# First FFN product of two half layers by quarters, with seven products for eight

## The chip, the cores and the metric

The kernel runs on one core of a Trainium2 chip. Its time is the device time of one execution in microseconds (us); lower is better. TensorE (PE) multiplies, VectorE (DVE) and ScalarE (ACT) work elementwise, GpSimd (POOL) and SyncE (SP) issue DMAs here.

## The reference, cut to what matters

A decoder of two layers, one with retention and one with sliding-window attention, runs one step for a prompt of 1024 tokens and a sample of 8 × 4 tokens. Each layer ends with a feed-forward part (FFN); the model's width is 1024, the FFN's 4096, all in float32.

```python
def rms_norm(x, g):
    xf = x.astype(jnp.float32)
    y = xf * lax.rsqrt(jnp.mean(xf * xf, axis=-1, keepdims=True) + EPS)
    return y.astype(x.dtype) * g.astype(x.dtype)

def ffn(h, g_pre, w1, w2, g_post):
    u = jax.nn.relu(rms_norm(h, g_pre) @ w1)
    return h + rms_norm((u * u) @ w2, g_post)
```

## The kernel before, in words

Activations lie feature by feature: 128 features on the partitions, tokens along the columns. Tokens go in two halves: half 0 has 512 (one piece), half 1 has 544 (two pieces of 272, the sample's 32 among them). A float32 product is made of three passes of a rounded format: each operand is split into a high part (a cast) and a low part (the rest), and `passes` (L343) gives high·high, high·low and low·high. Every accumulation over 1024 inputs is thus 8 × 3 matmuls.

`load_w` (L309) brings weights: for each block two DMAs of 128 x 1024 on SP's queue (L318), a cast on ScalarE for `whi` (L328), a subtraction on VectorE for `wlo` (L329). `proj_fm` (L346) multiplies: the matmul is L356, and after each pair of inputs it calls `tick` (L359).

`Ffn.up(i)` (L740) makes 256 of the 4096 features: two columns of 128, in half 0 as 2 × 24 = 48 matmuls of 512 columns, in half 1 as 96 of 272; ScalarE takes Relu out of PSUM (L748) and squares (L749), POOL stores the block to DRAM (`uD`, L751). `ups(a, b)` runs blocks a to b-1 of 16. `Ffn.downs` is the second product: it fetches `uD` by POOL (L756), cuts it into high and low parts (L763, L764), multiplies through `proj_fm`, and sums chunks on VectorE (`acc_out`, L362 to L367). PSUM has one pool: four banks tagged mm, four tagged aux.

The order of the work is the program's, with side work woven in. A side is a generator, such as `norms` (L280: it fetches `h` by POOL, takes `norm_r` with two matmuls by ones at L265 and L266, VectorE and ScalarE passes, and makes the next input's high part at L305 and its low part at L306). `tick` adds the work's size times a rate from the table `RATES` (L156) and runs a step of the first side for each whole unit; `drain` runs what is left. A scheduler may still shift instructions when the program is built. Around the change the main order is: the retention layer, in whose last part blocks 0 to 2 of `f0` run; then `f0` (half 0, layer 0), `f1` (half 1, layer 0), `fa` (half 0, layer 1) and `f2` (half 1, layer 1), each ups and then downs. Beside `f1.downs` and `fa.downs` run the sides of the attention of half 0 and half 1 (`at`, `smp`, `wo`, `lt`), whose last one makes the input of the next FFN. Beside `f0.ups` runs `norms` of half 1 (side f0), and beside `f2.ups` the norm and the output of half 0 (sides fo).

Of the kernel before, what the change touches and what calls it, by code (L numbers as in the profile page):

```python
# [116 lines left out]
def body(ctx, tc,  # L117
# [31 lines left out]
    def yt(w=TM, dt=F32):
        return yp.tile([P, w], dt, tag="y", bufs=16, name="y")  # L150
# [10 lines left out]
    def side(gen, rate=None):  # L161
        sides.append((gen, rate))
# [88 lines left out]
    def norm_r(get, w):  # L251
# [95 lines left out]
    def passes(a, b):  # L347
        return [(a[0], b[0]), (a[0], b[1]), (a[1], b[0])]
# [383 lines left out]
    class Ffn:  # L732
# [6 lines left out]
        def up(self, i):  # L739
# [10 lines left out]
            s_ = 2 * (i % 2)  # L750
            G.dma_start(out=uD[self.half][:, 2 * i:2 * i + 2], in_=self.st[:, s_:s_ + 2, :t_])  # L751

        def fetch(self, j):
            hi, lo = x4(), x4()
            t_ = TT[self.half]
            G.dma_start(out=f32(lo)[:, :, :t_], in_=uD[self.half][:, 4 * j:4 * j + 4])  # L756
            self.parts[j] = (hi, lo)

        def cut(self, j):
            t_ = TT[self.half]  # L760
            hi, lo = (t[:, :, :t_] for t in self.parts[j])
# [450 lines left out]
            S.activation(out=sel[:, i], in_=sel[:, i], func=AF.Copy, scale=den[:, i:i + 1])  # L1212

    def swa_sides(sw, half, am=None, skr=None):
        xs = []

        def late():
            xs.extend(xs_alloc())
            yield from norms(half, sw.y, g_spost, xs=xs, pre=g_f1)

        side(sw.attend(), f"at{half}")
        if half:
            side(sw.attend_sample(am, skr), "smp")
        side(sw.wo(), f"wo{half}")
        side(late(), f"lt{half}")
        return xs

    CHUNKS = [1, 2, 2, 2, 1]
    with tc.tile_pool(name="rp", bufs=1) as rp:
        G.dma_start(out=g_first, in_=gsrcs[0].rearrange("(k p) -> p k", p=P))  # L1230
# [4 lines left out]
        rets = [Ret(0, [(hi[k // 4][:, k % 4], lo[k // 4][:, k % 4]) for k in range(KT)], rp), None]  # L1235
        for _ in range(RATES["w0"]):
            next(ini)
        first = rets[0].qk_w(0, 0)
        run(ini)
        for g in (gen, x_store(0, loads), x_store(1)):  # L1240
            side(g, "x")
        qk = rets[0].qk(0, [[(0, 256)], [(256, 256)]], first)
        drain()
        prev = None
        for half in range(2):
            r = rets[half]
            for h in range(RH):
                pace[0] = RATES["vg"][half]
                last = h == RH - 1
                vs = r.v(h)  # L1250
                if last:
                    drain()
                    prev[0].wout(*prev[1:])
                    prev = None
                    xs = xs_alloc()
                    norm = norms(1 - half, xs=xs, pre=g_f0 if half else g_rpre)
                    side(norm, "n1")
                sg = r.g(h)
# [111 lines left out]
```

## Time and profile before

| | us |
|---|---|
| three runs | 2905.68, 2906.42, 2906.97 (median 2906.42) |
| profiled execution, its own time | 2905.74 |
| its span, first to last instruction | 2903.9 |
| TensorE busy in the span | 2849.2 |
| VectorE busy | 1526.7 |
| ScalarE busy | 1264.1 |

The profile lists for each group of instructions its line, engine, operation and tile, output <- input, with the partitions and columns. A busy time is the union of the instructions' own times; matmuls overlap one another, so the distance from start to start is shorter than the duration of one. A granted clock of 1.00 is 2.4 GHz, of 0.50 is 1.2 GHz. In a timeline, square brackets give the idle time of the engine before the row and what ended it.

### The profile page before, as it was taken

What the parts mean: (1) busy time and instruction counts of PE and PEld (TensorE: products, weight loads), DVE (VectorE), ACT (ScalarE), POOL (GpSimd) and SP (SyncE); (2) the same over time, 40 slices, a digit from 0 to 9 for tenths busy, and PEclk for the clock granted to TensorE, in tenths of its full rate; (3) what the DMA queues carried; (4) which work ended last, traced back from release to release, by engine and by line L of the source; (5) the groups of instructions that cost most, each with busy time, mean ns of one, the idle gap of its engine ahead of it and who ended that gap; (6) DMA issues with size and microseconds to landing.
All of it is one profiled execution on the core that took longest, in us unless ns stands there. A gap on an engine that the chain in (4) does not pass through costs nothing.

```text
span 2903.9 us, 42531 instructions
## 1 busy us (share of the span) xinstructions
PE 2849.2 (98%) x16989; PEld 2487.6 (86%) x16989; DVE 1526.7 (53%) x3045; ACT 1264.1 (44%) x2554; POOL 177.3 (6%) x262
## 2 busy tenths in 40 slices
PE   8999999999999999999999999999999999899998
PEld 7888888888989788888998898978877788899998
DVE  5444565576566644553444664654357535542345
ACT  3343353343325444432545764445458533444322
POOL 2000000011010100000000000000010100000000
PEclk9999999999999999999999999999999999899999
DMA  6322332455263645553554333355432434346432
GB/s 206 93 83 89 95 113 87 157 169 176 91 209 97 219 144 173 179 152 98 163 165 131 126 96 95 109 164 163 156 128 87 131 94 150 105 148 217 157 103 68
DMA packets 418420, 391.08 MB, mean 135 GB/s; under 512 B 13878, under 2 KB 360286, under 8 KB 416174
## 3 DMA queue, kind: packets, MB, share of 16 engines
q1 hardware_dynamic: 380191, 248.97, 29.0%
q0 software_dynamic: 36848, 137.36, 13.3%
q8 instruction: 133, 2.18, 0.3%
q10 hardware_dynamic: 1183, 2.04, 0.2%
q14 instruction: 65, 0.53, 0.1%
HBM read 308.73 MB, written 79.56 MB: 134 GB/s over the span
## 4 chain that ended last, share of the span: by engine, by line
PE 88%; issue 4%; DVE 3%; DMA 2%; ACT 2%; POOL 0%; SPq 0%; DVEq 0%; ACTq 0%; POOLq 0%
PE mm L356 66%; PE mm L496 6%; PE mm L940 5%; PE aux L629 2%; PE aux L638 2%; DMA wraw<-in_ffn_w_dram 1%; PE aux L705 1%; PE aux L1098 1%; PE aux L714 1%; PE aux L547 1%; PE aux L573 1%; PE aux L1065 1%; PE aux L496 1%; DVE wlo L329 0%; ACT whi L328 0%
## 5 line engine op out<-in xcount | busy, mean ns | idle before, releaser
L356 PE MATMUL mm<-x,whi 128*128 128x272 f32 (+2 forms) x8768 | 1912.6, 325 | 11.9 <-DVE y L367 6.0
L356 PEld LDWEIGHTS mm<-x,whi 128*128 128x128 f32 x8768 | 1381.7, 189 | 153.3 <-issue 9.8
L356 PE MATMUL mm<-x,wlo 128*128 128x272 f32 (+2 forms) x4384 | 1192.5, 324 | 0.0
L329 DVE TENSOR_TENSOR wlo<-wraw,whi 128x1024 fp32r<-128x1024 f32 x396 | 483.7, 1222 | 713.4 <-ACT whi L328 712.8
L328 ACT CAST whi<-wraw 128x1024 fp32r<-128x1024 f32 x396 | 415.4, 1049 | 938.2 <-PE mm L356 798.1
L356 PEld LDWEIGHTS mm<-x,wlo 128*128 128x128 f32 x4384 | 738.4, 189 | 62.1 <-DVE wlo L329 0.6
L367 DVE TENSOR_TENSOR y<-y,mm 128x272 f32<-128x272 f32 (+1 forms) x264 | 130.9, 516 | 182.5 <-PE mm L356 182.0
L496 PE MATMUL mm<-whi,x 128*128 128x512 f32 x512 | 166.9, 397 | 0.0
L940 PE MATMUL mm<-whi,x 128*128 128x512 f32 x384 | 124.2, 394 | 0.0
L496 PEld LDWEIGHTS mm<-whi,x 128*128 128x128 f32 x512 | 96.1, 189 | 22.8 <-DVE n L476 0.8
L496 PE MATMUL mm<-wlo,x 128*128 128x512 f32 x256 | 101.2, 395 | 0.0
L764 DVE TENSOR_TENSOR x<-x,x 128x1024 fp32r<-128x1024 f32 (+1 forms) x64 | 78.7, 1254 | 32.3 <-ACT x L763 32.1
L257 DVE TENSOR_TENSOR n<-n 128x272 f32<-128x272 f32 (+1 forms) x196 | 84.2, 430 | 10.7 <-ACT n L256 2.4
L749 ACT ACTIVATE x<-x 128x272 f32<-128x272 f32 (+1 forms) x192 | 88.5, 497 | 1.5
L940 PEld LDWEIGHTS mm<-whi,x 128*128 128x128 f32 x384 | 72.1, 188 | 17.6
L751 POOL DMA_DIRECT2D uD<-x x64 | 40.2, 628 | 746.4 <-ACT x L749 655.6
L748 ACT ACTIVATE x<-mm 128x272 f32<-128x272 f32 (+1 forms) x192 | 81.3, 457 | 3.6 <-PE mm L356 3.5
L763 ACT CAST x<-x 128x1024 fp32r<-128x1024 f32 (+1 forms) x64 | 66.8, 1076 | 22.1 <-DMA x<-uD 15.2
L940 PE MATMUL mm<-wlo,x 128*128 128x512 f32 x192 | 75.7, 394 | 0.0
L334 DVE SCALAR_TENSOR_TENSOR wlo<-wraw,gall,whi 128x512 fp32r<-128x512 f32 x48 | 34.6, 747 | 59.8 <-ACT whi L333 59.6
L496 PEld LDWEIGHTS mm<-wlo,x 128*128 128x128 f32 x256 | 48.4, 189 | 10.5
L333 ACT ACTIVATE whi<-wraw,gall 128x512 fp32r<-128x512 f32 x48 | 32.7, 717 | 54.5 <-PE aux L940 19.8
(310 smaller groups left out, 2531.8 us busy)
## 6 DMA issues: line engine op xcount, KB each, us to landing
wraw<-in_ffn_w_dram SPq DMA_DIRECT2D x256, 512.0 KB, 4.1
wraw<-in_ret_w_in_dram SPq DMA_DIRECT2D x96, 512.0 KB, 3.8
uD<-x POOLq DMA_DIRECT2D x32, 544.0 KB, 5.7
x<-uD POOLq DMA_DIRECT2D x16, 1088.0 KB, 7.4
wraw<-in_ret_w_out_dram SPq DMA_DIRECT2D x32, 512.0 KB, 3.5
x<-in_state_ret_dram SPq DMA_DIRECT2D x32, 512.0 KB, 5.3
out_dram<-x POOLq DMA_DIRECT2D x32, 512.0 KB, 3.4
uD<-x POOLq DMA_DIRECT2D x32, 512.0 KB, 5.7
```

The costliest lines, as they stand in the source:

```text
L257: V.tensor_tensor(out=acc, in0=acc, in1=sq, op=ALU.add)
L328: S.copy(out=hi, in_=raw)
L329: V.tensor_tensor(out=lo, in0=raw, in1=f32(hi), op=ALU.subtract)
L356: T.matmul(p_[:, :w], lhsT=a, rhs=b[:, o:o + w], start=(k == 0 and i == 0), stop=(k == n - 1 and i == 2))
L367: V.tensor_tensor(out=y[m][:, o:o + w], in0=y[m][:, o:o + w], in1=ps, op=ALU.add)
L496: T.matmul(ps[c][:a.shape[1]], lhsT=a, rhs=b, start=(k == 0 and i == 0), stop=(k == KT - 1 and i == len(prods) - 1))
L629: T.matmul(ps, lhsT=a, rhs=b, start=(n == 0), stop=(n == len(prods) - 1))
L748: S.activation(out=d, in_=ps, func=AF.Relu)
L749: S.activation(out=d, in_=d, func=AF.Square)
L763: S.copy(out=hi[:, a:a + 2], in_=f32(lo)[:, a:a + 2])
L764: V.tensor_tensor(out=lo[:, a:a + 2], in0=f32(lo)[:, a:a + 2], in1=f32(hi)[:, a:a + 2], op=ALU.subtract)
L940: T.matmul(ps[c][:a.shape[1]], lhsT=a, rhs=b, start=(k == 0 and i == 0), stop=(k == KT - 1 and i == len(prods) - 1))
```

## The change

The first FFN product of `f0` for blocks 5 to 15, and of `f2` for blocks 2 to 15, is made by another scheme (Winograd's form of Strassen's). A block's weights (1024 inputs, 256 features) and its input (1024 inputs, one half's tokens) are cut in quarters, A11 to A22 of the input by tokens (256 or 272 columns) and by inputs (512), and B11 to B22 of the weights. Seven products of 512 inputs, 128 features and 256 or 272 tokens replace eight. Each takes 4 × 3 = 12 matmuls, so a block takes 84. `Quarters.build` makes the sums S1 to S4 of the input once per half (14 VectorE operations and 4 casts, each of 1024 or 1088 columns) as a side `s7` during the two plain blocks ahead. `Seven` loads raw weights into a rotating tile (L354) and makes the sums T1, T3, T2 and T4 for each block: low parts at L370, sums at L373 (VectorE), casts on ScalarE at L377 (ha), L380 (h2), L387 (h1), L393 (hb) and L398 (h4). `seven` (L413) runs the products (matmul L429) and combines them: a copy u1 of the first product on ScalarE (L434), then on VectorE slot 0 (L437), slot 1 (L441), slot 2 (L444) and u2 (L446). `up7` takes Relu (L935) and Square (L936) of the whole block and stores it (L937). The blocks have a PSUM pool of their own, in which each product's tile has a single buffer: p1, px (two products), py (three) and p4.

The side f0 moves from `f0.ups` to `f0.downs`, the sides fo from `f2.ups` to `f2.downs`, and some rates change. In the new kernel `norm_r`'s matmuls are L272 and L273, `load_w`'s subtraction is L500 and `proj_fm`'s matmul L527.

```diff
-    RATES = {..., 'f0': 0.43, ..., 'at0': 2.4, 'wo0': 2.4, 'lt0': 2.4, 'at1': 3.25, 'smp': 3.25, 'wo1': 3.25, 'lt1': 3.25, 'fo': 0.43, ...}
+    RATES = {..., 'f0': 0.9, 's7': 1.25, ..., 'at0': 2.6, 'wo0': 2.6, 'lt0': 2.6, 'at1': 3.8, 'smp': 3.8, 'wo1': 3.8, 'lt1': 3.8, 'fo': 0.9, ...}
+    class Quarters:
...
+            def diff(r, a, b):
+                (ah, al), (bh, bl) = f[a], f[b]
+                V.tensor_tensor(out=r, in0=f32(ah), in1=f32(bh), op=ALU.subtract)
+                V.tensor_tensor(out=r, in0=r, in1=f32(al), op=ALU.add)
+                V.tensor_tensor(out=r, in0=r, in1=f32(bl), op=ALU.subtract)
...
+            diff(r0, "A22", "A21")
+            yield
+            minus(r1, r0, "A11")
+            yield
+            cut("S1", r0)
+            yield
+            minus(r0, r1, "A12")
+            cut("S2", r1)
+            yield
+            diff(r1, "A11", "A21")
+            yield
+            cut("S4", r0)
+            cut("S3", r1)
+            yield
...
+        def prep(self):
...
+            ha, la = pair()
+            f["B11"], f["B21"] = (ha[:, 0:4], la[:, 0:4]), (ha[:, 4:8], la[:, 4:8])
+            S.copy(out=ha, in_=raw[:, 0])
+            yield
+            h2, l2 = quarter("B22")
+            S.copy(out=h2, in_=b22)
+            low(ha, la, raw[:, 0])
+            yield
+            low(h2, l2, b22)
+            add(b11, b11, b12)
+            yield
+            h1, l1 = quarter("T1")
+            S.copy(out=h1, in_=b11)
+            add(b12, b12, b22)
+            add(b22, b11, b22)
+            yield
+            hb, lb = pair()
+            f["T3"], f["T2"] = (hb[:, 0:4], lb[:, 0:4]), (hb[:, 4:8], lb[:, 4:8])
+            S.copy(out=hb, in_=raw[:, 1])
+            add(b21, b22, b21)
+            low(h1, l1, b11)
+            yield
+            h4, l4 = quarter("T4")
+            S.copy(out=h4, in_=b21)
+            low(hb, lb, raw[:, 1])
+            yield
+            low(h4, l4, b21)
+            yield
...
+        p1 = pool.tile([P, 512], F32, tag="p1", name="p1")[:, :s]
+        px = pool.tile([P, 2, 512], F32, tag="px", name="px")[:, :, :s]
+        py = pool.tile([P, 3, 512], F32, tag="py", name="py")[:, :, :s]
+        p4 = pool.tile([P, 512], F32, tag="p4", name="p4")[:, :s]
...
+        prod(p1, "A11", "B11")
+        u1 = c[:, 3, :s]
+        S.copy(out=u1, in_=p1)
+        prod(px[:, 1], "S2", "T2")
+        prod(px[:, 0], "A12", "B21")
+        V.tensor_tensor(out=slot(0), in0=twice(u1), in1=px, op=ALU.add)
+        u2 = c[:, 0, s:2 * s]
+        prod(py[:, 1], "S3", "T3")
+        prod(py[:, 2], "S1", "T1")
+        V.tensor_tensor(out=slot(1), in0=twice(u2), in1=py[:, 1:3], op=ALU.add)
+        u3, v = c[:, 1, :s], c[:, 1, s:2 * s]
+        prod(py[:, 0], "S4", "B22")
+        V.scalar_tensor_tensor(out=slot(2), in0=twice(v), scalar=-1.0, in1=py[:, 0:2], op0=ALU.mult, op1=ALU.subtract)
+        prod(p4, "A22", "T4")
+        V.tensor_tensor(out=u2, in0=u3, in1=p4, op=ALU.add)
...
+        def ups7(self, a, b):
+
+            self.xq = Quarters(self.half, self.xs)
+            side(self.xq.build(), "s7")
...
+            self.up(a - 2)
+            w = [load(a)]
+            self.up(a - 1)
+            drain()
+            run(w[0].prep())
+            w.append(load(a + 1))
+            bank_pool("p7")
+            for i in range(a, b):
+                if i + 2 < b:
+                    w.append(load(i + 2))
+                if i == b - 2:
+                    self.fetch(0)
+                self.up7(i, w[i - a], w[i + 1 - a] if i + 1 < b else None)
+            bank_pool("pp")
+            self.cut(0)
...
+        f0.ups7(5, 2 * NFB)
         xs = xs_alloc()
         side(norms(1, rets[1].y, g_rpost, xs=xs, pre=g_f0), "f0")
-        f0.ups(3, 2 * NFB)
         f0.downs(CHUNKS)
...
-        f2.ups(0, 1)
+        f2.ups7(2, 2 * NFB)
...
-        f2.ups(1, 2 * NFB)
         f2.downs([2, 2, 2, 1])
```

First place: VectorE in the up blocks of `f0`. Before, it stands between norm steps (L257, L262, L303, L306) and the low parts of weights (L329):

```order
L329 TENSOR_TENSOR wlo<-wraw,whi 128x1024
L262 TENSOR_TENSOR n<-n 128x272
L329 TENSOR_TENSOR wlo<-wraw,whi 128x1024 x9
L269 TENSOR_TENSOR n<-n 128x272
L270 SCALAR_TENSOR_TENSOR n<-aux,n 128x272
L271 SCALAR_TENSOR_TENSOR n<-n 128x272
L303 SCALAR_TENSOR_TENSOR n<-x_9579,gall,n 128x272 x8
```

Now one block's rows, from its slot 0 on (x_9867 is the result, x_9736 the next block's raw weights, x_9860 those of the one after it):

```order
L437 TENSOR_TENSOR x_9867<-x_9867,px 128x512
L370 TENSOR_TENSOR wlo<-x_9736,whi 128x1024
L370 TENSOR_TENSOR wlo<-x_9860,whi 128x1024
L370 TENSOR_TENSOR y<-x_9736,y 128x512
L441 TENSOR_TENSOR x_9867<-x_9867,py 128x512
L373 TENSOR_TENSOR x_9860<-x_9860 128x512
L370 TENSOR_TENSOR y<-x_9736,y 128x512
L446 TENSOR_TENSOR x_9867<-x_9867,p_9866 128x256
L373 TENSOR_TENSOR x_9860<-x_9860 128x512
L444 SCALAR_TENSOR_TENSOR x_9867<-x_9867,py 128x512
L370 TENSOR_TENSOR y<-x_9860,y 128x512
L373 TENSOR_TENSOR x_9860<-x_9860 128x512 x2
```

Thirteen operations stand in one queue for each block; slot 1 (L441) has three low parts ahead of it: lb and l1 of the next block and la of the one after.

Second place: TensorE from one seven-product block to the next, in `f0` (p_10235 is the next block's p1, x_9566 is S4, x_9564 is S2):

```order
L429 MATMUL p_10235<-x_8290,whi 128x256
L429 MATMUL p_10235<-x_8292,whi 128x256
L429 MATMUL p_10235<-x_8290,wlo 128x256
L429 MATMUL py<-x_9566,y 128x256 x12
L429 MATMUL p_10235<-x_8290,whi 128x256
L429 MATMUL p_10235<-x_8292,whi 128x256
L429 MATMUL p_10235<-x_8290,wlo 128x256
L429 MATMUL p_10235<-x_8290,whi 128x256
L429 MATMUL p_10235<-x_8292,whi 128x256
L429 MATMUL p_10235<-x_8290,wlo 128x256
L429 MATMUL px<-x_9564,whi 128x256 x2
```

The product S4 of a block stands in the middle of P1 of the next one; before, a block was 48 matmuls of 512 columns at L356 with no other between.

Third place: TensorE where `fa.downs` (512 columns) meets `f2` (272 columns). Before, the two matmuls of the last norm stand inside `f2.up(0)`:

```order
L356 MATMUL mm<-x_22306,whi 128x272
L356 MATMUL mm<-x_22308,whi 128x272
L356 MATMUL mm<-x_22306,wlo 128x272
L265 MATMUL aux<-n,onesd 128x272
L266 MATMUL aux<-n,onesd 128x272
L356 MATMUL mm<-x_22305,whi 128x272 x3
```

Now they stand inside the last down product:

```order
L272 MATMUL aux<-n,onesd 128x272
L527 MATMUL mm<-x_22788,whi 128x512
L527 MATMUL mm<-x_22789,whi 128x512
L273 MATMUL aux<-n,onesd 128x272
L527 MATMUL mm<-x_22788,wlo 128x512
```

Behind L273 come 13 matmuls of 512 columns and then the first of 272. After that norm's first pair of matmuls came 174 matmuls of `fa.downs` before and 258 now; where `f1.downs` meets `fa`, 44 of 272 columns came after the last pair and 116 now.

## Rows read from the trace of the kernel before

**Rows 1.** The page: busy time of each engine, and the chain of waits by engine.
```profile
PE 2849.2 (98%) x16989; PEld 2487.6 (86%) x16989; DVE 1526.7 (53%) x3045; ACT 1264.1 (44%) x2554; POOL 177.3 (6%) x262
...
PE 88%; issue 4%; DVE 3%; DMA 2%; ACT 2%; POOL 0%; SPq 0%; DVEq 0%; ACTq 0%; POOLq 0%
```

**Rows 2.** Windows of up blocks: us, busy PE, PEld, DVE, ACT, POOL, clock, DMA share, GB/s.
```profile
1050.92:1174.03 123.11, 123.11 (x533) 99.52 (x533) 53.28 (x80) 62.39 (x99) 11.94 (x17) 1.00 0.58 183
2515.63:2688.07 172.44, 172.44 (x1383) 172.44 (x1382) 56.43 (x78) 75.31 (x163) 10.50 (x19) 1.00 0.54 175
```

**Rows 3.** Timeline of TensorE at the start: start us, duration, engine, line, tile, count.
```profile
26.44 0.40 PE L356 MATMUL mm<-x,whi 128*128 128x256 f32 x2
...
28.56 0.40 PE L356 MATMUL mm<-x,whi 128*128 128x256 f32 x2
```

**Rows 4.** Windows of two boundaries: before f2, before fa.
```profile
2444.90:2502.00 57.10, 41.36 (x206) 35.75 (x205) 43.93 (x95) 25.22 (x56) 2.64 (x3) 0.82 0.43 131
1860.00:1917.70 57.70, 51.50 (x351) 48.12 (x350) 47.43 (x112) 26.88 (x58) 2.28 (x3) 0.97 0.43 134
```

**Rows 5.** Timeline of ScalarE and TensorE before f2.
```profile
2466.88 1.04 ACT L328 CAST whi<-wraw 128x1024 fp32r<-128x1024 f32 x1 [8.25 <-DMA wraw<-in_ffn_w_dram]
...
2468.30 0.60 PE L265 MATMUL aux<-n,onesd 128*128 128x272 f32 x1 [3.86 <-ACT n L261]
...
2485.17 0.59 PE L265 MATMUL aux<-n,onesd 128*128 128x272 f32 x1 [8.89 <-ACT n L261]
...
2489.23 1.27 PE L356 MATMUL mm<-x,whi 128*128 128x272 f32 x4 [2.99 <-ACT x L305]
```

**Rows 6.** Timeline of TensorE before fa.
```profile
1887.35 0.52 PE L356 MATMUL mm<-x,whi 128*128 128x272 f32 x2 [1.73 <-DVE y L367]
...
1903.73 0.70 PE L356 MATMUL mm<-x,whi 128*128 128x512 f32 x2 [3.87 <-DVE y L367]
```

**Rows 7.** Timeline of f2's up blocks: a norm matmul and ScalarE behind it.
```profile
2602.17 0.28 PE L266 MATMUL aux<-n,onesd 128*128 128x256 f32 x1
...
2602.49 0.47 ACT L268 ACTIVATE n<-aux,epsc 128x256 f32<-128x256 f32 x1 [2.74 <-PE aux L266]
```

**Rows 8.** Timeline of VectorE: operations of one kind without a wait between.
```profile
621.80 2.47 DVE L505 TENSOR_TENSOR x<-mm,y 128x512 fp32r<-128x512 f32 x4
...
1249.57 2.35 DVE L764 TENSOR_TENSOR x<-x,x 128x1024 fp32r<-128x1024 f32 x2
```

**Rows 9.** Groups by line and form: busy us, mean ns of one, idle before.
```profile
L356 PEld LDWEIGHTS mm<-x,whi 128*128 128x128 f32 x8768 | 1381.7, 189 | 153.3 <-issue 9.8 <-ACT n L256 4.1 <-ACT x L305 4.0
...
L329 DVE TENSOR_TENSOR wlo<-wraw,whi 128x1024 fp32r<-128x1024 f32 x396 | 483.7, 1222 | 713.4 <-ACT whi L328 712.8
L328 ACT CAST whi<-wraw 128x1024 fp32r<-128x1024 f32 x396 | 415.4, 1049 | 938.2 <-PE mm L356 798.1 <-PE mm L496 53.2 <-PE aux L496 27.6
...
L367 DVE TENSOR_TENSOR y<-y,mm 128x512 f32<-128x512 f32 x88 | 60.2, 685 | 89.0 <-PE mm L356 88.8
...
L748 ACT ACTIVATE x<-mm 128x512 f32<-128x512 f32 x64 | 37.9, 591 | 0.1
```

**Rows 10.** Windows with dense side work, columns as in rows 2.
```profile
2180.00:2200.00 20.00, 20.00 (x105) 15.18 (x104) 17.32 (x42) 19.89 (x53) 0.75 (x1) 1.00 0.28 82
1620.00:1640.00 20.00, 18.14 (x137) 16.18 (x136) 16.91 (x36) 18.40 (x48) 0.00 (x0) 1.00 0.21 64
1880.00:1900.00 20.00, 18.14 (x143) 17.70 (x142) 19.46 (x49) 7.72 (x17) 1.76 (x2) 1.00 0.52 167
```

**Rows 11.** The page's DMA issues: KB each, us from issue to landing.
```profile
uD<-x POOLq DMA_DIRECT2D x32, 544.0 KB, 5.7
```

**Rows 12.** Window of line 356 alone: us, busy PE, PEld, clock, DMA.
```profile
2490.00:2495.00 5.00, 5.00 (x24) 5.00 (x23) 0.50 0.01 3
```

**Rows 13.** Window behind attention, columns as in rows 2.
```profile
2325.00:2330.00 5.00, 5.00 (x20) 3.77 (x20) 2.36 (x6) 1.81 (x5) 0.00 (x0) 0.69 0.11 23
```

**Rows 14.** Window at the program's start, columns as in rows 2.
```profile
30.00:40.00 10.00, 10.00 (x88) 10.00 (x87) 8.65 (x19) 3.42 (x5) 1.72 (x3) 1.00 0.36 111
```

More of the change, by code (lines that the diff above doesn't have):

```diff
@@ L272, in norm_r, with __init__, fill @@
         return t
-    def xs_alloc():
-        hi, lo = [x4(), x4()], [x4(), x4()]
-        return [(hi[k // 4][:, k % 4], lo[k // 4][:, k % 4]) for k in range(KT)]
+    class Parts(list):
+        def __init__(self, hi=None, lo=None):
+            if hi:
+                self.fill(hi, lo)
+        def fill(self, hi, lo):
+            self.extend((hi[k // 4][:, k % 4], lo[k // 4][:, k % 4]) for k in range(KT))
+            self.hi, self.lo = hi, lo
+    def xs_alloc():
+        return Parts([x4(), x4()], [x4(), x4()])
@@ new lines, in body, with __init__, pair, quarter @@
+    class Seven:
+        def __init__(self, src):
+            self.raw = x4(F32).rearrange("p a b -> p (a b)")[:, :2048].rearrange("p (i k c) -> p i k c", i=2, k=8)
+            for i in range(2):
+                nc.sync.dma_start(out=self.raw[:, i], in_=src[:, i * P:(i + 1) * P].rearrange("(k p) c -> p k c", p=P))
+            self.f = {}
+        def prep(self):
+            raw, f = self.raw, self.f
+            b11, b21, b12, b22 = raw[:, 0, 0:4], raw[:, 0, 4:8], raw[:, 1, 0:4], raw[:, 1, 4:8]
+            def pair():
+                return [wp.tile([P, 1024], F32R, tag=g, bufs=WB, name=g).rearrange("p (k c) -> p k c", k=8)
+                        for g in ("whi", "wlo")]
+            def quarter(n):
+                f[n] = [yt(TM, F32R)[:, :512].rearrange("p (k c) -> p k c", k=4) for _ in range(2)]
+                return f[n]
+            def low(h, l, r):
+                V.tensor_tensor(out=l, in0=r, in1=f32(h), op=ALU.subtract)
+            def add(r, a, b):
+                V.tensor_tensor(out=r, in0=a, in1=b, op=ALU.add)
+            ha, la = pair()
[26 more added lines that the diff above has]
+            yield
+        def rows(self, n):
+            h, l = self.f[n]
+            return [(h[:, k], l[:, k]) for k in range(4)]
@@ new lines, in seven, with slot, twice, prod @@
+    def seven(xq, wq, after):
+        s = xq.s
+        pool = banks[1]
+        p1 = pool.tile([P, 512], F32, tag="p1", name="p1")[:, :s]
+        px = pool.tile([P, 2, 512], F32, tag="px", name="px")[:, :, :s]
+        py = pool.tile([P, 3, 512], F32, tag="py", name="py")[:, :, :s]
+        p4 = pool.tile([P, 512], F32, tag="p4", name="p4")[:, :s]
+        c = x4(F32)
+        def slot(i):
+            return c[:, i, :2 * s].rearrange("p (a t) -> p a t", a=2)
+        def twice(ap):
+            return ap.unsqueeze(1).to_broadcast([P, 2, s])
+        def prod(ps, a, b):
+            A, B = xq.rows(a), wq.rows(b)
+            for k in range(4):
+                for i, (w_, x_) in enumerate(passes(B[k], A[k])):
+                    T.matmul(ps, lhsT=w_, rhs=x_, start=k == 0 and i == 0, stop=k == 3 and i == 2)
+            after()
+        prod(p1, "A11", "B11")
[13 more added lines that the diff above has]
+        V.tensor_tensor(out=u2, in0=u3, in1=p4, op=ALU.add)
+        return c
@@ L751, in up, with up7, after, load @@
             G.dma_start(out=uD[self.half][:, 2 * i:2 * i + 2], in_=self.st[:, s_:s_ + 2, :t_])
+        def up7(self, i, wq, nxt):
+            t_ = TT[self.half]
+            steps = nxt.prep() if nxt else iter(())
+            def after():
+                next(steps, None)
+            c = seven(self.xq, wq, after)
+            run(steps)
+            d = c.rearrange("p (a b) t -> p a b t", b=2)[:, :, 0, :t_]
+            S.activation(out=d, in_=d, func=AF.Relu)
+            S.activation(out=d, in_=d, func=AF.Square)
+            G.dma_start(out=uD[self.half][:, 2 * i:2 * i + 2], in_=d)
+        def ups7(self, a, b):
+            self.xq = Quarters(self.half, self.xs)
+            side(self.xq.build(), "s7")
+            def load(i):
+                return Seven(ffn_w1[self.l][:, i * 256:(i + 1) * 256])
+            self.up(a - 2)
[11 more added lines that the diff above has]
+                self.up7(i, w[i - a], w[i + 1 - a] if i + 1 < b else None)
+            bank_pool("pp")
+            self.cut(0)
+            self.xq = None
         def fetch(self, j):
@@ L1214, in swa_sides @@
     def swa_sides(sw, half, am=None, skr=None):
-        xs = []
+        xs = Parts()
         def late():
-            xs.extend(xs_alloc())
+            xs.fill([x4(), x4()], [x4(), x4()])
             yield from norms(half, sw.y, g_spost, xs=xs, pre=g_f1)
@@ L1234, in body @@
         loads = next(ini)
-        rets = [Ret(0, [(hi[k // 4][:, k % 4], lo[k // 4][:, k % 4]) for k in range(KT)], rp), None]
+        rets = [Ret(0, Parts(hi, lo), rp), None]
         for _ in range(RATES["w0"]):
```

36 lines of the change are left out of this document (32 added, 4 removed).

## The prediction

> **What bounds the kernel now.** The page's engine shares come first: TensorE is busy 98% of the span and makes 88% of the chain of waits [rows 1]. So the time is TensorE's stream and its gaps; what VectorE and ScalarE do beside it costs nothing until TensorE waits for it. The windows of two stretches of up blocks show that stream without a gap and at a granted clock of 1.00, the 2.4 GHz level: 533 matmuls, nearly all of 512 columns, in 123.11 us in half 0, so 0.231 each; 1383, nearly all of 272, in 172.44 us in half 1, 0.1247 each; VectorE is busy 43% and 33%, ScalarE 51% and 44% [rows 2]. The timeline of the program's start has matmuls of 256 columns, 18 from 26.44 to 28.56, 0.118 each [rows 3]. Last, two places where the next layer's input is made beside down products, by windows, show what TensorE loses [rows 4]. Before f2, 57.10 us stand where 96 matmuls of 512 columns, 96 of 272 and some 0.7 of norms need 22.2 + 12.0 + 0.7 = 34.9: 22 are lost, 15.7 of them idle (57.10 − 41.36), with waits of 3.86, 8.89 and 2.99 for the norm [rows 5], and 6.4 at the low clock. Before fa, 57.70 stand for 290 matmuls of 272, 48 of 512 columns and 0.5 of norms, 47.8: some 9 to 10 are lost, over half in two waits (1.73 and 3.87) for VectorE's accumulation [rows 6].
>
> **The change, part by part.** *TensorE's work.* A block of 256 features takes 48 × 0.231 = 11.09 us in half 0 and 96 × 0.1247 = 11.97 in half 1. Seven products of 4 × 3 matmuls are 84: at 0.118, 9.91 us; at 0.1247, 10.47. With 11 and 14 such blocks TensorE alone would save 11 × 1.18 + 14 × 1.50 = **34.0 us**, the upper end.
>
> *What paces a block.* Each of the four PSUM tiles has one buffer, and the order ties the engines in a ring. S4 of a block writes the tile that slot 1 reads; slot 1 stands on VectorE behind lb, la and l1 of the coming weights; la waits for ScalarE's cast ha, which may overwrite its buffer only when T3 has read it. So a turn is: T3's end to its waiter, 0.2 (an estimate: a norm's second matmul begins at 2602.17, ScalarE behind it at 2602.49 [rows 7], so 0.32 less the step of 0.12); the cast 1.05; a hand-off 0.05; la 1.14; l1 0.60; slot 1 0.69; a hand-off 0.04; then 12 matmuls of S4, the six that P1 still has, and the 36 of T2, B21 and T3. The VectorE prices are steps between operations in a row [rows 8]: two of 1024 take 2.35 us where one takes 1.22 [rows 9], so the second adds 1.13; four of 512 take 2.47 where one takes 0.685, so each further one 0.60. Half 0: 3.77 + 54 × 0.118 = **10.14 us**. Half 1, with slots of 544 (0.73 by width) and 55 matmuls: 3.81 + 55 × 0.1247 = **10.67**. Savings: 11 × 0.95 + 14 × 1.30 = **28.7 us**. VectorE's own sum per block is 2 × 1.14 + 10 × 0.60 + 0.34 = 8.6 (u2, half as wide, by proportion 0.34); ScalarE's is 2 × 1.05 for casts of 1024, at most 4 × 0.6 for three of 512 and the copy (a Relu of 512 takes 0.591), and about 2 × 1.05 for Relu and Square of 1024, 6.6 [rows 9]. Neither fills the ring alone. The ends of this price: 34.0 where the queues slip past each other, and 14.8, the first rival.
>
> The Trainium skill ("VectorE: DVE Perf Modes", section "The DRAIN you can't avoid") says that the next VectorE operation starts only when the pipe of the one before is empty; by that, la and l1 would cost 1.22 and 0.685, each turn 0.17 more and the 25 blocks 4 us more, about 2869. The rows disagree: four operations end 0.27 before four full durations would [rows 8, 9]. I keep the steps.
>
> *Starts and ends of these stretches.* The first product waits until Relu of the last plain block has freed PSUM, 0.59 [rows 9] and hand-offs, 0.75. The first down matmul waits until the last block's PSUM is read: 0.2 + 0.69 + 0.2 = 1.1, once in each half. Together **3.0 us** lost. The start in half 1 is counted with its boundary, next.
>
> *The boundary before f2.* The norm's side work runs at 3.8 for 3.25. Its last pair of matmuls then has 13 matmuls of 512 columns behind it instead of standing inside up(0), and 258 down matmuls instead of 174 follow the first pair: 84 × 0.231 = 19.4 us more cover, against waits of 15.7. If these go, the low clock behind them goes too. New there: up(0) still meets the last pieces of x as they are made (half of the wait of 2.99 there now, 1.5). VectorE then has 14 operations for S1 to S4 at about 1.2 (16.8), four low parts of plain weights (4.6) and the first block's weights (6.5), 27.9, of which two plain blocks cover 24; with a last cast TensorE waits some 4.3. Two PSUM hand-overs cost 0.6 each and a dozen matmuls at the low clock 1.2. That is 8.2 of loss in place of 22. Gain 13.8, of which I take **12**; ends 4 (the faster side work waits for ScalarE, where the wait of 8.25 for a weight's DMA stands in the same place [rows 5]) and 17 (the new waits hardly come).
>
> *The boundary before fa.* The last pair moves up by 72 matmuls of 272 columns, 9 us, against 9 to 10 lost. VectorE is busy 19.46 of 20 us there [rows 10], so some stays: gain **6**, ends 0 and 9.
>
> *The attention before that* is squeezed into less time: with ScalarE busy 19.89 of 20 TensorE is still full, at 18.40 in another stretch it idles 1.86 [rows 10]. One such stretch more in each of the two layers is 3.7: loss **3**, ends 0 and 5.
>
> *Moved at no cost.* Norms 1 and the output's last stage go from up to down products, which hold the same matmuls with VectorE about half idle; without that cover they are a drain of a few us at each end. The weights' DMAs through SP carry the same bytes per block. POOL stores the result from one of two tiles; the copy u1 waits for the store of two blocks before, which lands 5.7 us after its issue [rows 11], against 20 us between.
>
> **The sum.** 28.7 − 3.0 + 12 + 6 − 3 = 40.7 us. The profiled run took 2905.74, so 2865.0; the median of the runs is 0.7 higher, which changes nothing at this size: **2865**.
>
> **The rivals.** *VectorE paces the blocks.* If each operation costs its full duration (2 × 1.22 + 10 × 0.685 + 0.42 = 9.7) and six waits for TensorE or ScalarE at 0.2 are not hidden, a block takes 10.9, in half 1 with its wider slots 11.1: 11 × 0.2 + 14 × 0.9 = 14.8 in place of 28.7, so 2879. For it: a block's operations are one queue in order. Against: the steps [rows 8]. Chance 0.10.
>
> *The boundaries give nothing.* Faster rates bring side work forward only if ScalarE and VectorE have time; they may simply wait. Then 12 and 6 go: 2883. For it: VectorE's 19.46 of 20. Chance 0.09.
>
> *The clock falls in the blocks: slower.* Single-buffered PSUM makes TensorE stop and go in every turn. At the low level, 1.2 GHz, 24 records of 272 columns touch a stretch of 5 us at a clock of 0.50 [rows 12], some 0.22 each, so 84 take 18.5 us. For it: 5 us with TensorE busy throughout and narrow matmuls at a mean clock of 0.69 [rows 13]. Against: 1.00 over a stretch with 9% idle [rows 10]. Each such block costs 8.1 us; from five of the 25 on, the gain of 41 is gone. Eight give 2930. Chance 0.05.
>
> *Weight loads show: slower.* Half 0 loads weights for every 256 columns where it now does for 512, and a load is listed with 0.189 us [rows 9], more than a step of 0.118. If one load hides under one matmul only, a step is 0.189, a block 15.9, and 11 of them cost 63 us more than forecast: 2928. It decides from 45 ns on each of the 924 matmuls (41 us). Against: 88 matmuls with 87 loads stand in 10.00 us at the start, mostly of 256 columns [rows 14]. Chance 0.02. The Trainium skill ("TensorE: Matmul & The Clock Gate", section "The mechanism") lets a load overlap matmuls in flight only where the row groups differ, which full-height loads never do, and elsewhere on that page puts a load of 128 columns at 107 ns; by that the 924 would add some 99 us. The row of the start excludes it.
>
> *No effect*: what the blocks gain is cancelled within 6 us by their starts, the waits for the sums of x and the squeezed side work. Chance 0.04.
>
> **How the numbers follow.** The forecast holds 0.70, with a range of its own from 2846 (34, 17 and 9 gained, starts and attention nearly hidden) to 2883 (blocks 25, boundaries 4 and 2, attention 5). The range to 2892 takes in the first two rivals with the lower ends of the rest; the slower rivals and no effect stay out. A measurement of this kernel can tell 0.2%, about 6 us, from no change. Faster: 0.70 + 0.10 + 0.09 = 0.89; within 0.2%: 0.04; slower: 0.05 + 0.02 = 0.07.
>
> **What would show it.** In the profile after: 84 matmuls per 10.1 us in half 0's seven-product stretch and per 10.7 in half 1's, with TensorE's wait ahead of S4, released by VectorE's slot 1; steps of 0.118 and a clock of 1.00; the waits of 3.86, 8.89, 2.99 and 3.87 gone, with some 4 us of waits for S1 to S4 in their place. The prediction is wrong if VectorE is busy without a gap in the blocks, if a granted clock below 1 stands there, or if idle time of 15 us still precedes f2.

## The result and the profile after

The changed kernel took 2874.28 us (median of four runs, 2868.01 to 2876.51) against 2906.05; the ratio is 0.9889, interval 0.9871 to 0.9908. Run again in a later series (e9) it took 2874.26 (2869.18 to 2877.69), ratio 0.9900, interval 0.9886 to 0.9913. The forecast was 2865 in a range from 2846 to 2892: the direction and the size hold, and the median is 9 us above the point. The profiled execution took 2868.01, the fastest of its four, and is the one shown unless another is named; the one of the later series took 2873.69.

The page of the kernel after, engine shares and chain by engine; they answer to [rows 1]:

```profile
PE 2815.8 (98%) x17217; PEld 2474.9 (86%) x17217; DVE 1725.0 (60%) x3348; ACT 1319.3 (46%) x2556; POOL 180.6 (6%) x262
...
PE 87%; issue 5%; DVE 4%; ACT 2%; DMA 2%; POOL 0%; SPq 0%; DVEq 0%; ACTq 0%; POOLq 0%
```

TensorE's busy time is 33 us shorter and VectorE's 198 longer, and the kernel is bound as before.

The turn of a seven-product block can be read from the copy u1, one for each block. The timeline of ScalarE in the kernel after, second and tenth block of `f0`, second and thirteenth of `f2`:

```profile
1059.92 0.37 ACT L434 COPY x<-p 128x256 f32<-128x256 f32 x1
...
1141.07 0.37 ACT L434 COPY x<-p 128x256 f32<-128x256 f32 x1 [0.26 <-PE p L429]
...
2505.64 0.39 ACT L434 COPY x<-p 128x272 f32<-128x272 f32 x1 [0.85 <-PE p L429]
...
2623.30 0.39 ACT L434 COPY x<-p 128x272 f32<-128x272 f32 x1 [0.44 <-PE p L429]
```

A turn is the time from one u1 to the next. Eight turns in 81.15 us are **10.14** each, eleven in 117.66 are **10.70**; forecast were 10.14 and 10.67. The windows of the two stretches, columns as in [rows 2]:

```profile
1059.92:1141.07 81.15, 81.15 (x675) 79.92 (x674) 73.09 (x106) 50.98 (x66) 6.57 (x9) 1.00 0.51 156
2505.64:2623.30 117.66, 117.65 (x926) 116.66 (x925) 103.27 (x150) 71.49 (x89) 8.44 (x12) 1.00 0.49 152
```

The clock is 1.00. TensorE seems busy throughout, since the listed durations of its matmuls reach over the gaps; the weight loads' column shows the gap, 1.23 us over eight turns, 0.15 each. The timeline of all engines over one turn shows the ring, with slot 1 (L441) ahead of S4:

```profile
1084.27 1.06 ACT L377 CAST whi<-x 128x1024 fp32r<-128x1024 f32 x1 [0.36 <-PE py L429]
...
1085.36 1.23 DVE L370 TENSOR_TENSOR wlo<-x,whi 128x1024 fp32r<-128x1024 f32 x1 [0.19 <-ACT whi L377]
...
1086.51 0.68 DVE L370 TENSOR_TENSOR y<-x,y 128x512 fp32r<-128x512 f32 x1
...
1087.11 0.68 DVE L441 TENSOR_TENSOR x<-x,py 128x512 f32<-128x512 f32 x1
...
1087.84 1.49 PEld L429 LDWEIGHTS py<-x,y 128*128 128x128 f32 x12 [0.15 <-DVE x L441]
```

The cast ha waits for T3, la for the cast, l1 and slot 1 for la, and S4 for slot 1: the steps of the prediction, in its order.

Stage lengths from event to event show where the rest went. An event is the first Relu of an FFN's up blocks or the first copy of its down sums on ScalarE; a stage runs from one to the next. The columns e3 to e8 are experiments that the next section tells.

| us, profiled execution | before | change | e3 | e4 | e7 | e8 |
|---|---|---|---|---|---|---|
| f0 ups | 231.1 | 218.8 | 218.8 | 231.6 | 218.9 | 217.0 |
| f0 downs | 180.1 | 183.3 | 183.3 | 179.6 | 183.3 | 183.3 |
| f1 ups | 258.8 | 258.8 | 258.8 | 258.8 | 258.8 | 258.8 |
| f1 downs, attention 0, start of fa | 295.7 | 298.5 | 302.5 | 296.2 | 301.2 | 300.2 |
| fa ups | 257.3 | 257.4 | 257.4 | 257.3 | 257.3 | 257.3 |
| fa downs, attention 1, start of f2 | 307.2 | 307.0 | 316.3 | 308.2 | 308.5 | 309.6 |
| f2 ups | 216.1 | 183.7 | 184.4 | 199.0 | 177.8 | 175.0 |
| f2 downs to the end | 211.5 | 213.5 | 213.7 | 211.1 | 213.3 | 213.5 |

The change's column sums to 36.8 less than before, and 1.1 less stood ahead of `f0` in that execution. `f0` as a whole gives 9.1 (norm work moved from ups to downs); `fa` downs and `f2` as a whole give 30.6; the stage from `f1`'s downs to `fa` costs 2.8. That last number is the smallest of its kind: in the ten profiles of kernels with the change's rates beside `f1`'s downs the stage took 298.5 to 303.2, 301.4 on average, so 5.7 more than before. The idle time of TensorE in the kernel after, from its timeline, where it answers to [rows 5, 6]:

```profile
1048.21 0.51 PE L429 MATMUL p<-x,whi 128*128 128x256 f32 x2 [0.69 <-ACT x L919]
...
1160.91 0.70 PE L527 MATMUL mm<-x,whi 128*128 128x512 f32 x2 [0.87 <-DVE x L444]
...
1856.41 0.49 PE L527 MATMUL mm<-x,whi 128*128 128x272 f32 x2 [3.23 <-DVE y L538]
...
1872.84 0.51 PE L527 MATMUL mm<-x,whi 128*128 128x272 f32 x2 [0.90 <-DVE y L538]
...
1887.46 0.52 PE L527 MATMUL mm<-x,whi 128*128 128x272 f32 x2 [2.09 <-DVE y L538]
...
2485.69 0.52 PE L429 MATMUL p<-x,whi 128*128 128x272 f32 x2 [0.65 <-ACT x L919]
...
2492.61 0.82 PE L429 MATMUL px<-x,whi 128*128 128x272 f32 x2 [5.14 <-ACT whi L393]
...
2644.19 0.74 PE L527 MATMUL mm<-x,whi 128*128 128x272 f32 x4 [1.07 <-DVE x L446]
```

Before `f2` the waits of 3.86, 8.89 and 2.99 are gone, and one of 5.14 for the first block's weights is there. Before `fa` the waits of 0.60, 1.73 and 3.87 became 3.23, 0.90 and 2.09: the same sum, 6.2, earlier. The first of the old ones, from the timeline of the kernel before:

```profile
1877.36 0.38 PE L265 MATMUL aux<-n,onesd 128*128 128x256 f32 x1 [0.60 <-ACT n L261]
```

### The profile page after: what moved, and what is told of

Same layout as the page of the kernel before. It is cut to its first block, busy times and chain, and to the rows that moved or that the text cites. A ratio compares the mean times of both kernels' runs of the same rounds, so it can differ in the third digit from the quotient of the medians.

```text
span 2866.2 us, 43419 instructions
## 1 busy us (share of the span) xinstructions
PE 2815.8 (98%) x17217; PEld 2474.9 (86%) x17217; DVE 1725.0 (60%) x3348; ACT 1319.3 (46%) x2556; POOL 180.6 (6%) x262
## 4 chain that ended last, share of the span: by engine, by line
PE 87%; issue 5%; DVE 4%; ACT 2%; DMA 2%; POOL 0%; SPq 0%; DVEq 0%; ACTq 0%; POOLq 0%
PE mm L527 57%; PE mm L667 6%; PE mm L1151 4%; PE py L429 4%; PE px L429 3%; PE p L429 2%; PE aux L800 2%; PE aux L809 2%; PE aux L876 1%; PE aux L1309 1%; DVE wlo L500 1%; PE aux L885 1%; PE aux L718 1%; PE aux L744 1%; PE aux L1276 1%
## 5 line engine op out<-in xcount | busy, mean ns | idle before, releaser
L527 PE MATMUL mm<-x,whi 128*128 128x272 f32 (+2 forms) x7520 | 1652.3, 326 | 11.2 <-DVE y L538 6.2
L527 PEld LDWEIGHTS mm<-x,whi 128*128 128x128 f32 x7520 | 1189.1, 189 | 136.0 <-issue 10.2
L527 PE MATMUL mm<-x,wlo 128*128 128x272 f32 (+2 forms) x3760 | 1030.8, 325 | 0.6 <-DVE wlo L500 0.5
L500 DVE TENSOR_TENSOR wlo<-wraw,whi 128x1024 fp32r<-128x1024 f32 x346 | 422.8, 1223 | 474.6 <-ACT whi L499 474.0
L527 PEld LDWEIGHTS mm<-x,wlo 128*128 128x128 f32 x3760 | 635.2, 189 | 55.7 <-DVE wlo L500 1.5
L429 PE MATMUL py<-x,y 128*128 128x272 f32 (+1 forms) x600 | 84.1, 289 | 0.2 <-DVE x L441 0.2
L429 PE MATMUL px<-x,whi 128*128 128x272 f32 (+1 forms) x400 | 75.5, 287 | 5.1 <-ACT whi L393 5.1
L429 PEld LDWEIGHTS py<-x,y 128*128 128x128 f32 x600 | 76.4, 188 | 3.0 <-DVE x L441 1.8
L370 DVE TENSOR_TENSOR wlo<-x,whi 128x1024 fp32r<-128x1024 f32 x50 | 61.1, 1225 | 15.6 <-ACT whi L377 10.7
L373 DVE TENSOR_TENSOR x<-x 128x512 f32<-128x512 f32 x100 | 68.9, 689 | 1.6
```

The costliest lines, as they stand in the source:

```text
L370: V.tensor_tensor(out=l, in0=r, in1=f32(h), op=ALU.subtract)
L373: V.tensor_tensor(out=r, in0=a, in1=b, op=ALU.add)
L429: T.matmul(ps, lhsT=w_, rhs=x_, start=k == 0 and i == 0, stop=k == 3 and i == 2)
L500: V.tensor_tensor(out=lo, in0=raw, in1=f32(hi), op=ALU.subtract)
L527: T.matmul(p_[:, :w], lhsT=a, rhs=b[:, o:o + w], start=(k == 0 and i == 0), stop=(k == n - 1 and i == 2))
```

## The experiments

Each ran beside the kernel before on one chip; e1 to e4, e5 to e8 and e9 to e11 share one each.

**e1, S4 in a PSUM tile of its own.**

```diff
-        py = pool.tile([P, 3, 512], F32, tag="py", name="py")[:, :, :s]
+        py = pool.tile([P, 2, 512], F32, tag="py", name="py")[:, :, :s]
+        p0 = pool.tile([P, 512], F32, tag="p0", name="p0")[:, :s]
...
-        prod(py[:, 0], "S4", "B22")
-        V.scalar_tensor_tensor(out=slot(2), in0=twice(v), scalar=-1.0, in1=py[:, 0:2], op0=ALU.mult, op1=ALU.subtract)
+        V.scalar_tensor_tensor(out=c[:, 2, s:2 * s], in0=v, scalar=-1.0, in1=py[:, 0], op0=ALU.mult, op1=ALU.subtract)
+        prod(p0, "S4", "B22")
+        V.scalar_tensor_tensor(out=c[:, 2, :s], in0=v, scalar=-1.0, in1=p0, op0=ALU.mult, op1=ALU.subtract)
```

> The change with S4's product in a PSUM tile of its own, and slot 2 made as two operations of half the width. Ring theory: what sets a block's turn is slot 1, which S4 waits for only because both share a tile; with the tile split S4 no longer waits and a turn falls to TensorE's own 84 matmuls, from 10.14 to 9.92 us in half 0 and from 10.69 to 10.5 in half 1, some 5 us less than the change in all (11 x 0.22 + 14 x 0.19), although VectorE has 0.1 us more work per block. Rival (VectorE's queue paces the block): the turn stays at 10.14 and 10.69 or grows by the 0.1.

Measured: 2865.96 us, ratio 0.9870 (0.9855 to 0.9885). The copies u1 in e1, third and tenth block of `f0`:

```profile
1069.41 0.37 ACT L435 COPY x<-p 128x256 f32<-128x256 f32 x1 [0.97 <-PE p L430]
...
1139.05 0.37 ACT L435 COPY x<-p 128x256 f32<-128x256 f32 x1 [0.96 <-PE p L430]
```

Seven turns in 69.64 us are 9.95; in half 1 the usual turn is 10.54, with two longer (10.70 and 11.06), 10.60 on average. `f0`'s ups took 217.0 us and `f2`'s 179.5, together 6.0 less than in the change. VectorE has more to do for each block than in the change, and the turn still fell: so it was set by S4's wait for slot 1 through the shared tile, not by VectorE's total. Sharing the tile costs 0.1 to 0.2 us for each block.

**e2, the old rate beside `f1`'s downs** (`'at0': 2.4, 'wo0': 2.4, 'lt0': 2.4`).

> The change with the rates of at0, wo0 and lt0 back at 2.4. Theory: the faster side work beside f1.downs did not pay, since VectorE is full there and the down products' sums only queue behind the norm earlier; from the first down sum of f1 to the first Relu of fa it goes back from 298.5 us to about 295.7, the total is 2 to 3 us less than the change. Rival: the stretch is longer for another reason (the clock of that execution), and the time stays within 1 us of the change.

Measured: 2871.16 us, ratio 0.9888 (0.9873 to 0.9902); the stage 298.1 in its profile. Neither number settles it: the ratio is that of the change, and the stage is 2.4 above the 295.7 expected. e10 comes back to it.

**e3, the old rate beside `fa`'s downs** (`'at1': 3.25` and its three neighbours).

> The change with the rates of at1, smp, wo1 and lt1 back at 3.25. Theory: the boundary before f2 gained by the rate, so with the old one idle time of over 12 us ahead of f2 comes back, and the total is 8 to 14 us more than the change. Rival: the gain came from the other arrangement of f2's start (the output's side work moved away, two plain blocks ahead), and the total stays within 2 us.

Measured: 2884.14 us, ratio 0.9934 (0.9919 to 0.9949), 10 more than the change's median; in its profile `fa`'s downs are 9.3 longer. Two of the old waits are back in its timeline:

```profile
2473.53 0.59 PE L272 MATMUL aux<-n,onesd 128*128 128x272 f32 x1 [8.93 <-ACT n L268]
...
2477.59 0.82 PE L527 MATMUL mm<-x,whi 128*128 128x272 f32 x2 [2.99 <-ACT x L476]
```

**e4, the kernel before with that rate alone** (`'at1': 3.8` and its neighbours in the kernel before).

> The kernel before with nothing but the rates of at1, smp, wo1 and lt1 raised to 3.8. Theory: the three waits ahead of f2 (15.7 us) and the low clock behind them mostly go, with 1 to 2 us given back in the denser attention, so 10 to 18 us less than before without a single product saved. Rival: the rate pays only together with the seven products; then within 3 us of before.

Measured: 2888.97 us, ratio 0.9946 (0.9929 to 0.9962): **four numbers of the rate table give 15 us without a product saved**, where the whole change gives 32 and the same numbers inside it are worth 10 (e3). `f2`'s up blocks take 199.0 us in place of 216.1. The window over them in e4:

```profile
2477.80:2676.80 199.00, 199.00 (x1596) 199.00 (x1596) 68.34 (x99) 89.36 (x197) 12.54 (x22) 1.00 0.52 165
```

No idle time and a clock of 1.00, but the window begins behind a wait for the last pieces of x, from the same timeline of TensorE:

```profile
2475.38 0.51 PE L356 MATMUL mm<-x,whi 128*128 128x272 f32 x2 [2.62 <-ACT x L305]
```

So with plain blocks the start of `f2` costs 2.6 idle once the norm is early, where the change has no such wait, but 0.65 and 5.14 idle ahead of its first seven-product block. The gains are not a sum: the change without the rate (e3) gives 20, the rate alone 15, both together 32.

**e5 and e6, more work for VectorE.** In e5 the line `low(h1, l1, b11)`, in e6 the line `low(h2, l2, b22)` stands twice.

> The change with the low part l1 of T1 written twice for each block: one more VectorE operation of 512 columns (0.60 us), which stands behind slot 1 in VectorE's queue, outside the ring, in both halves. Ring theory: the turn of a block stays at 10.14 us in half 0 and 10.69 in half 1. Rival (VectorE's total sets the pace): 0.6 us more per block, 10.7 and 11.3.

> The change with the low part l2 of B22 written twice for each block: one more VectorE operation of 0.60 us; in half 0 the operation la of the block after next moves behind slot 1 in VectorE's queue, in half 1 it stays ahead of it. Ring theory: in half 0 slot 1 no longer waits for ScalarE's cast ha and for la, so a block gets faster by TensorE's whole wait, from 10.14 to 9.92 to 10.0 us, though VectorE does more; in half 1 it stays at 10.69. Rival (VectorE's total): 0.6 us more in both halves.

Measured in e5, 2869.51 us in one run: eight turns from 1059.94 to 1141.05, 10.14, and in half 1 10.69 in the later blocks (10.65 on average). VectorE's busy time in these eight turns rose to 77.48 of 81.11 us:

```profile
1059.94:1141.05 81.11, 81.11 (x675) 79.88 (x674) 77.48 (x113) 50.98 (x65) 6.56 (x9) 1.00 0.51 156
```

So 0.6 us more of VectorE per block cost nothing while it stood outside the ring. In e6, 2880.9 us in one run, half 1 stayed at 10.69 in its later blocks, but half 0 took 10.02 to 10.14 in its first four turns and 10.26 in the next five: neither the 9.92 to 10.0 of the theory nor the rival's 10.7. Its timeline of all engines says why for the later turns:

```profile
1114.21 0.69 DVE L438 TENSOR_TENSOR x<-x,px 128x512 f32<-128x512 f32 x1 [0.32 <-issue]
...
1114.82 1.41 DVE L373 TENSOR_TENSOR x<-x 128x512 f32<-128x512 f32 x2
...
1115.59 1.05 ACT L394 CAST whi<-x 128x1024 fp32r<-128x1024 f32 x1 [1.81 <-DVE x L373]
...
1116.67 1.23 DVE L370 TENSOR_TENSOR wlo<-x,whi 128x1024 fp32r<-128x1024 f32 x1 [0.45 <-ACT whi L394]
...
1117.82 0.68 DVE L442 TENSOR_TENSOR x<-x,py 128x512 f32<-128x512 f32 x1
...
1118.55 1.68 PE L430 MATMUL py<-x,y 128*128 128x256 f32 x12
```

With la behind slot 1, two sums had moved behind slot 0 as well, and another ring closes: px, slot 0, a sum, the cast hb, lb, slot 1, S4, the rest of P1, px. From 1114.21 to S4 are 4.34 us, and the time of some 47 matmuls follows. Half of my expectation fell: I had followed one operation's move, not the whole queue's.

**e7, three plain blocks ahead of `f2`'s seven-product blocks** (`f2.ups7(3, 2 * NFB, 3)`, the third argument being the number of plain blocks).

> The change with three plain blocks instead of two ahead of f2's seven-product blocks (13 of them for 14). Theory: the wait of 5.14 us for the first block's cast and the low clock after it (some 3.5 us over 5 us at 0.50 and 5 at 0.86) come from VectorE, which has 14 operations of 1.2 us and the first block's weights to do within two plain blocks; a third plain block (12.0 us against 10.69, so 1.3 more) covers them, and the total is 5 to 8 us less than the change. Rival: the side work only stretches to fill the third block, the wait stays, and the total is 1 us more.

Measured: 2866.16 us, ratio 0.9862 (0.9845 to 0.9878), 8 less than the change by the medians; in its profile `f2`'s ups are 5.9 shorter. The same place in the timeline of e7, and windows over it:

```profile
2503.16 0.52 PE L429 MATMUL p<-x,whi 128*128 128x272 f32 x2 [0.65 <-ACT x L919]
```

```profile
2500.00:2505.00 5.00, 4.35 (x35) 4.12 (x34) 4.06 (x7) 3.19 (x7) 0.53 (x1) 1.00 0.76 206
2505.00:2510.00 5.00, 4.78 (x37) 4.55 (x37) 4.81 (x7) 1.96 (x4) 0.00 (x0) 1.00 0.67 220
```

The hand-over of PSUM is left, the wait of 5.14 is gone, and the granted clock there is 1.00. In the change, windows of this place show the price of the wait, 0.50 and 0.86 in the clock's column:

```profile
2485.00:2490.00 5.00, 1.81 (x13) 1.55 (x12) 5.00 (x6) 2.19 (x6) 0.54 (x1) 0.96 0.92 272
2490.00:2495.00 5.00, 2.35 (x7) 1.77 (x8) 5.00 (x7) 4.11 (x6) 0.00 (x0) 0.50 0.15 43
2495.00:2500.00 5.00, 5.00 (x37) 5.00 (x36) 4.89 (x10) 0.18 (x1) 0.00 (x0) 0.86 0.62 167
```

VectorE is full there, as the theory had it.

**e8, e1 and e7 together.**

> S4's own PSUM tile and three plain blocks together. Theory: both gains add, 5 us for the tile and 5 to 8 for the plain block, so 10 to 13 us less than the change, about 2862. Rival: with a faster turn the first blocks' weights come too late and the two gains overlap, less than 6 us.

Measured: 2861.67 us, ratio 0.9851 (0.9836 to 0.9866), 12.6 below the change's median. In the profile `f0`'s and `f2`'s ups are 10.5 shorter than in the change, where e1 alone gave 6.0 and e7 5.9: most of both gains adds.

**e9 to e11, the change, e8 with the old rate of e2, and e8, on one chip.**

> The change as it is, beside the two below on one chip. Expected: 2868 to 2877 as in its first runs; from the first down sum of f1 to the first Relu of fa 298 to 303 us, with a granted clock below 1 in the attention's first 25 us in some executions.

> S4's own PSUM tile, three plain blocks, and the rates of at0, wo0 and lt0 back at 2.4. Theory: the faster side work beside f1.downs packs the attention's start, where TensorE waits more and the clock falls, and gains nothing at the boundary, so this stretch goes back to 296 to 298 us and the total is 2 to 5 us less than with the new rate, 2857 to 2860. Rival: the rate does nothing there, the total is within 1 us of the version with the new rate.

> S4's own PSUM tile and three plain blocks with the new rate of at0, beside e10 on one chip. Expected: 2860 to 2864; the stretch of f1 named there at 299 to 303 us.

Measured: 2874.26, 2859.92 and 2863.34 us. e10's five runs (2857.58 to 2861.34) all lie below e11's four (2863.01 to 2865.24): the faster side work beside `f1` costs 3.4 us. e10 has the lowest median of this study, ratio 0.9850 (0.9837 to 0.9864) to before and 14 us below the change. Windows over the first 25 us of attention 0, of e9, of e10, of e11 and of the change's first profile:

```profile
1607.03:1632.03 25.00, 22.12 (x144) 19.77 (x143) 18.50 (x39) 20.50 (x50) 0.00 (x0) 0.86 0.31 112
```

```profile
1605.33:1630.33 25.00, 22.98 (x176) 20.82 (x175) 20.48 (x46) 21.94 (x57) 0.00 (x0) 1.00 0.32 112
```

```profile
1605.28:1630.28 25.00, 22.13 (x143) 19.79 (x142) 18.49 (x39) 20.50 (x50) 0.00 (x0) 0.86 0.32 113
```

```profile
1606.05:1631.05 25.00, 22.11 (x166) 19.60 (x164) 20.55 (x46) 21.86 (x56) 0.00 (x0) 1.00 0.32 115
```

With the new rate TensorE is busy 0.9 us less there, and the clock was 0.86 in e9 and e11, though 1.00 in the first profile of the change: 144 matmuls in 25 us against 166. The stage from `f1` to `fa` took 298.5 in the execution of 2868.01 and 303.1 in that of 2873.69, so 4.6 of the 5.7 us between them lie in it; how much of this is the clock isn't shown. The profiled execution of e10 took 2861.34, above its median, and its stage has 301.0 against e11's 301.3, so where the 3.4 us lie isn't shown: the total is the theory's, the stretch is not. Nor is the rate the whole loss of this stage: with the old rate it took 298.1 in e2 and 301.0 in e10, where the kernel before has 295.7.

**e12, less work for VectorE before `fa`.**

```diff
-            V.tensor_tensor(out=acc, in0=acc, in1=sq, op=ALU.add)
+            if k == 1 or not thin[0]:
+                V.tensor_tensor(out=acc, in0=acc, in1=sq, op=ALU.add)
```

> The change with 24 VectorE operations of 256 columns left out of the norms beside f1.downs: of the eight squares only two are summed, so these norms' values are others. That is 24 x 0.335 = 8 us less for VectorE in the last 75 us before fa, where TensorE now idles 6.2 us. Theory (VectorE is full there, so faster side work only moves the wait): the idle time of these 75 us falls below 2.5 us and the total by 4 to 6 us against the change. Rival (the norm's chain of hand-offs between the engines sets the waits): the idle time stays at 5 us or more and the total within 2 us.

Measured: 2873.83 us, ratio 0.9896 (0.9879 to 0.9912), no change. The last 75 us before `fa` in e12:

```profile
1833.43:1858.43 25.00, 23.53 (x185) 22.97 (x184) 22.86 (x52) 15.24 (x34) 1.76 (x2) 1.00 0.43 126
1858.43:1883.43 25.00, 20.69 (x156) 20.45 (x155) 22.24 (x53) 10.22 (x23) 1.76 (x2) 0.94 0.54 172
1883.43:1908.43 25.00, 25.00 (x176) 23.75 (x175) 13.23 (x25) 7.86 (x12) 0.00 (x0) 0.99 0.38 106
```

VectorE is busy 58.3 us, where the change has 64.1, and TensorE idles 5.8, where the change has 6.2. So the theory falls, and both numbers are the rival's. VectorE's and TensorE's timelines in e12 show where the longest wait comes from:

```profile
1872.32 1.27 DVE L477 SCALAR_TENSOR_TENSOR n<-x,gall,n 128x256 f32<-128x256 f32 x3
...
1876.86 1.43 DVE L480 TENSOR_TENSOR x<-n,x 128x256 fp32r<-128x256 f32 x4 [2.14 <-ACT x L479]
...
1880.40 1.48 DVE L541 TENSOR_TENSOR y<-y,mm 128x272 f32<-128x272 f32 x4
...
1880.89 0.82 PE L530 MATMUL mm<-x,whi 128*128 128x272 f32 x2 [4.31 <-DVE y L541]
```

Sixteen operations that make the next input stand in one burst of 8.1 us, during which VectorE itself waits 2.14 for ScalarE, and the sums of the down products (L541) are queued behind it. TensorE goes on until a matmul needs a PSUM bank that those sums must read first, and waits 4.31. In the change's own timeline of VectorE 8.6 us lie between the start of such a burst and the first sum behind it, ahead of TensorE's wait of 3.23:

```profile
1847.23 1.28 DVE L474 SCALAR_TENSOR_TENSOR n<-x,gall,n 128x256 f32<-128x256 f32 x3
...
1855.83 0.44 DVE L538 TENSOR_TENSOR y<-y,mm 128x272 f32<-128x272 f32 x1
```

This points to the length of the burst, and less of VectorE's total changed nothing. That shorter bursts would remove the wait wasn't tried, so it isn't shown.

## Why the prediction came out, point by point

**The blocks** (28.7 forecast). By the turns measured, 11 × (11.09 − 10.14) + 14 × (11.97 − 10.70) = 28.2. The ring is shown by e1, which removes it, and by e5, which loads VectorE beside it. The rival that VectorE paces is out: 0.6 us more per block changed nothing. The clock was 1.00 but for the first block of `f2`, behind the wait of 5.14, and the weight loads stayed hidden as the row of the start had them.

**Starts and ends** (3.0 lost): 0.69, 0.87 and 1.07, so 2.6.

**The boundary before `f2`** (12 gained, and 1.5 lost in attention 1). `fa`'s downs and `f2` together gave 30.6; less 17.8 for 14 blocks and with 1.1 for their end that leaves 13.9, where 10.5 was forecast. The wait for the sums of the input and the first block's weights was put at 4.3 and is 5.14. e3 shows that 10.0 of the 13.9 hang on the rate, as the sum had it in the main (316.3 and 184.4 us with the old rate for 307.0 and 183.7, against 307.2 and 216.1 before); what gives the rest isn't shown. e7 shows that a third plain block makes `f2`'s ups 5.9 shorter.

**The boundary before `fa`** (6 gained, 1.5 lost in attention 0) is the step that failed. The stage got 2.8 us longer in the profile of 2868.01, 7.4 in that of 2873.69, so 7.3 and 11.9 us are missing against the forecast of 4.5 gained, where these executions lie 3.0 and 8.7 above 2865. The idle time ahead of `fa` kept its sum of 6.2, so the gain of 6 came to nothing, as the rival had it that the boundaries give nothing. Of the rest the windows show only a part: 0.9 us less of TensorE's work in the attention's first 25 us, and a clock of 0.86 there in the later profile; what makes the whole loss stays open. The range "0 to 9" had no loss in it. I had the row that spoke against the gain, VectorE busy 19.46 of 20 us, and read it as "some stays"; moved forward by 72 matmuls, the bursts only meet other sums. A full VectorE as the cause isn't borne out either: in e12 it had less to do and the idle time stayed. That the total of the profiled execution is only 3.0 off is partly luck: the 7.3 missing here and 0.5 in the blocks stand against 3.4 more before `f2`, 0.4 less at starts and ends, and 1.1 ahead of `f0` that no term held.

**No cost of moved work.** `f0`'s downs and `f2`'s downs got 3.2 and 2.0 longer. Of their 15 and 24 more TensorE records 4 each are matmuls of the norms that came with the side work; in `f2` the output's 32 transposes came too, and in `f0` the other 11 are down matmuls that now fall behind the event that opens the stage. The balance holds: `f0` as a whole gave 9.1 against 10.45 − 1.56 = 8.9 by the measured turns and ends.

## What to carry to other kernels

Where single-buffered tiles tie engines together, follow the ring from a release to the next one: its length is the turn, and work outside it is free (e5) as long as it doesn't reorder the queue into another ring (e6). Before crediting a scheme with a gain, run the old kernel with the new kernel's schedule numbers: here the schedule's numbers alone gave 15 us where the whole change gave 32. And where a short, urgent operation waits in a queue in order, look at the burst ahead of it and not only at busy shares: here a burst of 8.1 us stood ahead of a wait of 4.31.

## What the runs showed of the hardware

Back-to-back VectorE operations start closer together than one lasts. In the ring's timeline la starts 1.15 us before l1 and lasts 1.23, and l1 starts 0.60 before slot 1 and lasts 0.68; the turn is 10.14, as the steps have it, where full durations would make it 10.31. The Trainium skill ("VectorE: DVE Perf Modes", section "The DRAIN you can't avoid") says that the next operation waits until the pipe is empty, but also that "A next op that is not held starts earlier". The prediction named the first half alone; the steps agree with the second.

Weight loads stay hidden even where every matmul of 256 columns has its own: in e1, 84 matmuls with 84 loads take 9.95 us, 0.118 each, though a load is listed with 0.19.

The clock fell to 0.50 over 5 us that began within a wait of 5.14, and it stayed at 1.00 through turns with a gap of 0.15 in every 10.14. In the attention's start the same program had 1.00 in one execution and 0.86 in another; what decides between them these runs do not show.
